# Two more landing buffers for gathered expert rows, in place of a spare pair of split activations

## The chip, the cores and the metric

The kernel runs on one core of one Trainium2 chip. A core has five engines that run side by side, each with its own instruction stream: TensorE (PE, matrix products), VectorE (DVE), ScalarE (ACT), GpSimd (POOL) and SyncE (SP). SP issues most transfers, POOL the indirect ones (gathers), ACT a few; 16 DMA engines carry them. The metric is device microseconds of one execution, as the median of several.

## The reference

One layer of a hybrid encoder on 1024 tokens of width 1024, in float32. A first half mixes tokens (a causal convolution and an RWKV-7 state recurrence side by side, one output projection, residual, layer norm). The second half is PEER: each token chooses 16 experts for each of 8 heads out of 16384, and every expert is one row of `peer_u` and one of `peer_v`. This change touches only that second half:

```
s1, s2 = q_first_half . peer_k1, q_second_half . peer_k2       # 128 scores each, for a token and head
cand   = top16(s1)[:, None] + top16(s2)[None, :]               # 256 sums
sc, ci = top_k(cand, 16);  expert = i1 * 128 + i2;  gate = softmax(sc)
z   = einsum('td,tkd->tk', h, peer_u[expert])                  # 128 experts a token
y2  = einsum('tk,tkd->td', gelu(z) * gate, peer_v[expert])
x   = layer_norm(ALPHA * x + gate2 * y2, ln2_g, ln2_b)
```

## The kernel before

The tokens lie in eight tiles of 128. Five of them (`DT`, tiles 0 to 4, 640 tokens) are done *densely*: every expert is computed for every token, and a gate matrix that was built earlier holds a zero where a token did not choose an expert. Three tiles (`GT`, 5 to 7) are done by *gathering*: for each of a token's 128 experts its row is fetched. Both run together in the last stage, from about 1350 us to the end; all that goes before is left as it was.

**The dense part** goes through 32 groups of four chunks of 128 experts. For a chunk, a tile of `peer_u` is loaded (`uraw`) and split into two fp32r halves, `uhi` by ACT (L1301) and `ulo` by POOL (L1303). PE forms 2 x 24 "up" products (L1387) into PSUM banks `mg`; ACT applies the gelu (L1389), VectorE multiplies with the gates (L1391), and the result is split into `ah` (ACT, L1392) and `al` (VectorE, L1393). These pairs are 640 wide and come from a ring of `ABUF` = 6. When a group's four chunks are through, 120 "down" products (L1403) with the split `peer_v` tiles (`vhi`, `vlo`, again L1301 and L1303) go into three PSUM banks `md` in turn, and VectorE adds each bank to an accumulator `yacc` (L1421). The last group (`finish`) adds its banks to the residual tiles `xres` instead (L1354), takes statistics (L1355), normalizes (ACT, L1360), and multiplies and adds the layer norm's rows (L1361, L1362).

**The gathered part** is a generator, `gather(t)`, of which a step is made after each chunk and down tile, so that 256 gathers a tile spread over the groups. One gather is an indirect DMA issued by POOL (L1258) that lands 128 rows of 4 KB, one for each token of the tile, in a buffer `grow`. The first 128 of a tile are rows of `peer_u`: VectorE multiplies with the tokens `gh` and sums into a column of `z` (L1266). The other 128 are rows of `peer_v`: VectorE adds the row times its weight to `gy` in PSUM (L1273). Gather `k` is written ahead of the use of gather `k - 4` (`AHEAD`), and the ring `grow` has `GBUF` = 6 buffers, which the tokens, the residual tile and rows for the layer norm also take in turn. After the last addition the tile is scaled (L1276), added to the residual (L1226), normalized, multiplied and added to (L1230 on VectorE, L1232 on POOL) and stored (L1233).

**The late choices.** For tiles 6 and 7 the choice of experts is made inside this stage, by VectorE, piece by piece after an accumulation (`choose_late`, lines 953 to 963, L823 to L827 and `choose`), in memory of a pool of its own, `lt`. A tile's choices are finished before its gathers begin; the last end when the gathers of the second tile are under way.

**What sets the order.** The program is written in the order of the loops, but the instructions of each engine are put in order by a scheduler that simulates the program with the framework's own costs and buffer counts. So a change of a buffer count moves instructions on all engines from the place on where it first counts. Each engine then works strictly in its order, and so does SP's queue of transfers.

Of the kernel before, what the change touches and what calls it, by code (L numbers as in the profile page):

```python
# [10 lines left out]
F32 = mybir.dt.float32  # L11
# [11 lines left out]
D = 1024  # L23
# [20 lines left out]
REGIONS = [(0, 2, 16), (2, 2, 8), (4, 4, 4), (8, 8, 1)]  # L44
NCAND = sum(m * w for _, m, w in REGIONS)
TB = 32
GBUF = 6
AHEAD = 4
NMM = 3
AHEADF = 11,  # L50
MERGE = 7,
# [25 lines left out]
CBUF = 4  # L77
GB = 2, 3
MB = 3
ABUF = 6  # L80
VBUF = 4

PH = 4
# [13 lines left out]
def layer_kernel(ctx, tc, x, cols, c_row, cond_w, w_in, w2a2, g2, w_out, ln_rows, wq, keys, peer_u, peer_ut, peer_v, peer_vt, out):  # L97
# [185 lines left out]
    def drain(gen):  # L283
        for _ in gen:
            pass
# [296 lines left out]
    turn = [0, 0, 0]  # L582
# [46 lines left out]
    side, rate, credit, fills = [], [0.0], [0.0], [0]  # L629
# [21 lines left out]
    kept, ys, late, normed, page2, st3, blocks = {}, {}, [], {}, [], [], [0]  # L651
# [169 lines left out]
    def best16(vs, ix, sm):  # L821

        V.max(vs[:, 0:8], sm)  # L823
        V.max_index(ix[:, 0:8], vs[:, 0:8], sm)
        V.match_replace(sm, vs[:, 0:8], sm, -3.0e38)
        V.max(vs[:, 8:16], sm)
        V.max_index(ix[:, 8:16], vs[:, 8:16], sm)  # L827
# [125 lines left out]
    def choose_late(tt, lt):  # L953

        for g in range(4):
            s = lt.tile([128, 512], F32, name="lscore")
            ld(s, score_d[tt][g])
            vi = lt.tile([128, 128], F32, name="lvi").rearrange("p (q h a r) -> p q h a r", q=2, h=2, a=2)
            val, idx = vi[:, 0], vi[:, 1].bitcast(U32)
            for m in range(4):  # L960
                best16(val[:, m // 2, m % 2], idx[:, m // 2, m % 2], s[:, 128 * m:128 * m + 128])
                yield
            yield from choose(tt, val, idx, 2 * g, 2, 2, lambda nm, d, w: lt.tile([128, w], d, name="l" + nm), V)
# [234 lines left out]
    df = ctx.enter_context(tc.tile_pool(name="df", bufs=1))  # L1198
    dy = ctx.enter_context(tc.tile_pool(name="dy", bufs=1))
    gp = ctx.enter_context(tc.tile_pool(name="gp", bufs=1, side="right"))  # L1200
    lt = ctx.enter_context(tc.tile_pool(name="lt", bufs=1, side="right"))
    psd = ctx.enter_context(tc.tile_pool(name="psd", bufs=PSD, space=PSUM))
    psy = ctx.enter_context(tc.tile_pool(name="psy", bufs=1, space=PSUM))

# [7 lines left out]
    def grow(dt=F32):  # L1212
        return gp.tile([128, D], dt, name="grow", bufs=GBUF)

    def bcast_row(src):
        r = grow()
        ld(r, src[None, :].to_broadcast([128, D]))
        return r

    def residual_norm(t, acc):  # L1220

        xt = grow()
        ld(xt, x1_d[t])
        for i in range(2):
            h_ = slice(512 * i, 512 * i + 512)
            V.scalar_tensor_tensor(xt[:, h_], xt[:, h_], ALPHA, acc(i), op0=OP.mult, op1=OP.add)  # L1226
        parts = [xt[:, 0:512], xt[:, 512:1024]]
        normalize(parts, parts)
        r = bcast_row(ln_rows[2])
        V.tensor_mul(xt, xt, r)  # L1230
        r = bcast_row(ln_rows[3])
        G.tensor_add(xt, xt, r)  # L1232
        ld(out[128 * t:128 * t + 128], xt)  # L1233

    late = {t: choose_late(t, lt) for t in score_d}

    def gather(t):
        if t in late:
            drain(late.pop(t))
        sel = []  # L1240
        for w in range(3):
            s = gp.tile([128, 128], F32, name=f"gsel{w}")
            ld(s, sel_d[t][w])
            sel.append(s)
        eid = gp.tile([128, 128], I32, name="eid", bufs=2)
        V.scalar_tensor_tensor(eid, sel[0], 128.0, sel[1], op0=OP.mult, op1=OP.add)

        hs = grow()
        ld(hs, h2_d[t])
        ht = psy.tile([128, D], F32, tag="ghy", name="gh")  # L1250
        A.activation(ht, hs, AF.Copy)
        z = de.tile([128, 128], F32, name="gz")
        yield
        pend = []
        for k in range(256 + AHEAD):
            if k < 256:
                r = grow()
                G.indirect_dma_start(out=r, out_offset=None, in_=peer_u if k < 128 else peer_v,  # L1258
                                     in_offset=bass.IndirectOffsetOnAxis(ap=eid[:, k % 128:k % 128 + 1], axis=0))
                pend.append(r)  # L1260
            i = k - AHEAD
            if i < 0:
                continue
            r = pend.pop(0)
            if i < 128:
                V.scalar_tensor_tensor(r, r, 1.0, ht, op0=OP.mult, op1=OP.mult, accum_out=z[:, i:i + 1])  # L1266
            elif i == 128:
                A.activation(z, z, AF.Gelu)
                V.tensor_mul(z, z, sel[2])
                y = psy.tile([128, D], F32, tag="ghy", name="gy")  # L1270
                V.tensor_scalar(y, r, z[:, 0:1], None, op0=OP.mult)
            else:
                V.scalar_tensor_tensor(y, r, z[:, i - 128:i - 127], y, op0=OP.mult, op1=OP.add)  # L1273
            yield
        r = bcast_row(mod_d[5].rearrange("a b -> (a b)"))
        V.tensor_mul(y, y, r)  # L1276
        residual_norm(t, lambda i: y[:, 512 * i:512 * i + 512])
        yield


    side[:] = [gather(t) for t in GT]
    n_side = len(side) * (256 + 2)
    done = [0]
# [83 lines left out]
    for g in range(32):  # L1367
# [6 lines left out]
        for e in range(4):  # L1374
# [5 lines left out]

            ah, al = (dl.tile([128, ND], F32R, name=n_, bufs=ABUF) for n_ in ("ah", "al"))
            for bs in NBLK:
                p = md(NW) if g == 0 and e < 3 and bs.start else mg(NW)
                i = 0
# [95 lines left out]
```

## Time and profile before

| | |
|---|---|
| three runs | 3143.58, 3144.41, 3155.35 us; median 3144.41 |
| profiled execution | 3149.86 us, its span 3148.1 us, mean granted clock 0.965 |
| busy, share of the span | PE 94%, weight loads 83%, DVE 76%, ACT 37%, POOL 58% |
| DMA | 945.77 MB, mean 300 GB/s; 768 gathers bring 402.70 MB of it |
| chain that ended last | PE 56%, DVE 21%, DMA 9%, issue 6%, POOL 4%, ACT 4% |

The page groups instructions by line: how often, busy time, mean ns of one, and the idle time of the engine before them with what ended it. Idle time of an engine that is not the bottleneck costs nothing, so the view to read is the one of a stretch of time with the waits of PE in it. Matmuls overlap: a product's own duration is longer than the time from one to the next.

### The profile page before, as it was taken

Reading aid. Unit: us, or ns where it says so; the run is one execution under the profiler, and the core shown is the slowest. Engines: PE = TensorE matmul, PEld = TensorE weight load, DVE = VectorE, ACT = ScalarE, POOL = GpSimd, SP = SyncE. Lnnn points to the kernel's source line nnn. Section 1 sums busy time; section 2 is a strip of 40 time slices with the busy share of each in tenths; the row PEclk is TensorE's granted clock in tenths of the full one; section 3 lists DMA queues with packets and bytes.
Section 4 is the critical chain, followed back from the end, with each engine's and each line's share of the span. In section 5 each row is a group of like instructions: output and inputs, shape, how many; then the busy total and the mean of one; then the engine's idle time right before and its main releaser. Section 6 shows DMA issues by size and latency. Waiting matters only on the chain.

```text
span 3148.1 us, 54845 instructions
## 1 busy us (share of the span) xinstructions
PE 2954.2 (94%) x20416; PEld 2609.6 (83%) x20416; DVE 2383.7 (76%) x5388; ACT 1179.6 (37%) x2220; POOL 1814.5 (58%) x1419
## 2 busy tenths in 40 slices
PE   6979999989799889999999999999999999999996
PEld 4748667878678788899889888899898998999985
DVE  6276764437876989379999998887787877778789
ACT  5562452434345667732323323323232232222323
POOL 2434112224352443487777766877787677787874
PEclk9989999968888999999999999999999999999998
DMA  8878857768665887899999998999999989999995
GB/s 317 308 204 302 265 171 216 261 230 307 201 241 209 322 322 285 315 350 338 325 335 327 323 324 306 343 341 334 342 341 340 343 308 343 327 343 337 337 335 199
DMA packets 431851, 945.77 MB, mean 300 GB/s; under 512 B 92464, under 2 KB 234208, under 8 KB 411104
## 3 DMA queue, kind: packets, MB, share of 16 engines
q1 hardware_dynamic: 318112, 497.62, 46.9%
q0 software_dynamic: 110592, 402.70, 34.6%
q10 hardware_dynamic: 2880, 41.94, 3.3%
q8 instruction: 160, 2.62, 0.3%
q14 instruction: 107, 0.88, 0.1%
HBM read 800.76 MB, written 141.39 MB: 299 GB/s over the span
## 4 chain that ended last, share of the span: by engine, by line
PE 56%; DVE 21%; DMA 9%; issue 6%; POOL 4%; ACT 4%; SPq 1%; POOLq 0%; DVEq 0%; ACTq 0%
PE md L1403 18%; PE mg L1387 18%; PE mm L217 8%; DVE grow L1266 2%; PE mm L867 2%; PE mm L525 2%; DMA vraw<-peer_vt 2%; DVE gy L1273 2%; POOL grow L1258 2%; DMA cw<-cond_w 1%; PE mgate L1105 1%; DVE yacc L1421 1%; DVE mask L1091 1%; DMA grow<-peer_v,eid 1%; POOL ulo L1303 1%
## 5 line engine op out<-in xcount | busy, mean ns | idle before, releaser
L1387 PE MATMUL mg<-h2h,uhi 128*128 128x320 f32 x2024 | 627.1, 310 | 7.4 <-DVE al L1393 7.4
L1387 PE MATMUL mg<-h2h,ulo 128*128 128x320 f32 x2024 | 626.0, 309 | 4.6 <-POOL ulo L1303 4.5
L1387 PE MATMUL mg<-h2l,uhi 128*128 128x320 f32 x2024 | 626.1, 309 | 0.0
L1273 DVE SCALAR_TENSOR_TENSOR gy<-grow,gz,gy 128x1024 f32<-128x1024 f32 x381 | 487.5, 1279 | 28.6 <-DMA grow<-peer_v,eid 23.7
L1266 DVE SCALAR_TENSOR_TENSOR grow<-grow,gh 128x1024 f32<-128x1024 f32 x384 | 461.1, 1211 | 49.1 <-DMA grow<-peer_u,eid 38.7
L1403 PE MATMUL md<-vlo,ah 128*128 128x512 f32 x1260 | 491.1, 391 | 0.0
L1403 PE MATMUL md<-vhi,al 128*128 128x512 f32 x1260 | 490.7, 390 | 0.0
L1403 PE MATMUL md<-vhi,ah 128*128 128x512 f32 x1260 | 485.9, 392 | 4.5 <-ACT ah L1392 3.4
L1258 POOL DMA_INDIRECT grow<-peer_v,eid x384 | 367.5, 957 | 165.1 <-DVE gy L1273 58.3
L1258 POOL DMA_INDIRECT grow<-peer_u,eid x384 | 362.5, 944 | 172.3 <-issue 59.4
L1387 PEld LDWEIGHTS mg<-h2h,uhi 128*128 128x128 f32 x2024 | 380.5, 188 | 16.4 <-DVE al L1393 11.1
L1387 PEld LDWEIGHTS mg<-h2h,ulo 128*128 128x128 f32 x2024 | 380.5, 188 | 9.0 <-POOL ulo L1303 6.2
L1387 PEld LDWEIGHTS mg<-h2l,uhi 128*128 128x128 f32 x2024 | 380.5, 188 | 5.1
L1303 POOL TENSOR_TENSOR vlo<-vraw,vhi 128x1024 fp32r<-128x1024 f32 x128 | 308.7, 2412 | 64.2 <-ACT vhi L1301 62.1
L1301 ACT ACTIVATE vhi<-vraw 128x1024 fp32r<-128x1024 f32 x128 | 135.3, 1057 | 536.4 <-DMA vraw<-peer_vt 497.7
L1303 POOL TENSOR_TENSOR ulo<-uraw,uhi 128x1024 fp32r<-128x1024 f32 x128 | 309.4, 2417 | 26.1 <-ACT uhi L1301 19.2
L1403 PEld LDWEIGHTS md<-vhi,ah 128*128 128x128 f32 x1260 | 235.8, 188 | 53.6 <-ACT ah L1392 5.4
L1403 PEld LDWEIGHTS md<-vlo,ah 128*128 128x128 f32 x1260 | 236.5, 188 | 49.1
L1421 DVE TENSOR_TENSOR yacc<-md,yacc 128x512 f32<-128x512 f32 x300 | 203.9, 684 | 96.3 <-PE md L1403 87.0
L1098 POOL TENSOR_TENSOR ob<-mask,selt 128x384 f32<-128x384 bf16 x160 | 140.2, 890 | 233.9 <-DVE mask L1091 96.5
L1403 PEld LDWEIGHTS md<-vhi,al 128*128 128x128 f32 x1260 | 236.5, 188 | 44.9
L205 POOL TENSOR_TENSOR wsplit<-wraw,wsplit 128x1024 fp32r<-128x1024 f32 x46 | 112.5, 2448 | 215.7 <-ACT wsplit L204 193.9
(415 smaller groups left out, 5747.6 us busy)
## 6 DMA issues: line engine op xcount, KB each, us to landing
uraw<-peer_ut SPq DMA_DIRECT2D x128, 512.0 KB
vraw<-peer_vt SPq DMA_DIRECT2D x128, 512.0 KB
wsplit<-split_wq SPq DMA_DIRECT2D x48, 1024.0 KB
G_d<-stage ACTq DMA_DIRECT2D x20, 2048.0 KB
gmat<-G_d SPq DMA_DIRECT2D x32, 1024.0 KB
cw<-cond_w SPq DMA_DIRECT2D x48, 512.0 KB
wsplit<-split_w_out SPq DMA_DIRECT2D x24, 1024.0 KB
split_w_in<-wsplit SPq DMA_DIRECT2D x22, 1024.0 KB
```

What stands on the lines that cost most here:

```text
L205: G.tensor_sub(lo, raw, hi.bitcast(F32))
L217: T.matmul(pt, l[:, k, :], r[k], start=i == 0, stop=i == 3 * KD - 1)
L525: T.matmul(pt[:, 128 * g:128 * g + 128], dg[:, 128 * j:128 * j + 128], ubuf[ct][:, g, LAGS - 1 - m:LAGS - 1 - m + 128], start=m == 0, stop ...
L1098: G.tensor_mul(ob[:, :3], mb[:, :3], gt[:, c:c + 3, None].to_broadcast([128, 3, 128]))
L1258: G.indirect_dma_start(out=r, out_offset=None, in_=peer_u if k < 128 else peer_v, in_offset=bass.IndirectOffsetOnAxis(ap=eid[:, k % 128:k ...
L1266: V.scalar_tensor_tensor(r, r, 1.0, ht, op0=OP.mult, op1=OP.mult, accum_out=z[:, i:i + 1])
L1273: V.scalar_tensor_tensor(y, r, z[:, i - 128:i - 127], y, op0=OP.mult, op1=OP.add)
L1301: A.activation(hi, raw, AF.Copy)
L1303: G.tensor_sub(lo, raw, hi.bitcast(F32))
L1387: T.matmul(p, l[:, k, :], r[k][:, bs], start=i == 0, stop=i == 3 * KD - 1)
L1403: T.matmul(p, l[:, ts], r[:, e % 2, :], start=e == 0 and q == 0, stop=e == 3 and q == 2)
L1421: ins = V.tensor_add(ya, p, ya)
```

## The change

`ABUF` goes from 6 to 5, which frees one `ah` and one `al`. `GBUF` goes from 6 to 7. `AHEAD` goes; the loop keeps `GBUF - 1` gathers written ahead, counted with the one that is used next, so five beyond it for four before. When the last late choice has been taken in the program (`late` is empty), its pool `lt` is closed and a pool `gq` with one buffer, `gland`, is opened in its place. From then on every eighth gather lands there, and six stand ahead.

```diff
-GBUF = 6
-AHEAD = 4
+GBUF = 7
...
-ABUF = 6
+ABUF = 5
...
-    lt = ctx.enter_context(tc.tile_pool(name="lt", bufs=1, side="right"))
+    ltx = ctx.enter_context(ExitStack())
+    lt = ltx.enter_context(tc.tile_pool(name="lt", bufs=1, side="right"))
...
+    more, turn = [], [0]
+
+    def landing():
+
+        if not late and not more:
+            ltx.close()
+            more.append(ctx.enter_context(tc.tile_pool(name="gq", bufs=1, side="right")))
+        turn[0] += 1
+        if more and turn[0] % (GBUF + 1) == 0:
+            return more[0].tile([128, D], F32, name="gland")
+        return grow()
...
-        pend = []
-        for k in range(256 + AHEAD):
-            if k < 256:
-                r = grow()
+        pend, k = [], 0
+        for i in range(256):
+            while k < 256 and len(pend) < GBUF - 1 + len(more):
+                r = landing()
                 G.indirect_dma_start(out=r, out_offset=None, in_=peer_u if k < 128 else peer_v,
                                      in_offset=bass.IndirectOffsetOnAxis(ap=eid[:, k % 128:k % 128 + 1], axis=0))
                 pend.append(r)
-            i = k - AHEAD
-            if i < 0:
-                continue
+                k += 1
             r = pend.pop(0)
```

No instruction is added or taken away; 53 of the 768 gathers land in `gland`, of which the first is gather 352. Up to the first down products of the first group every engine has the same order in both programs. From there it differs, in small moves all along. Line numbers of the changed program are lower by one up to the new function and higher by nine behind it (L1258 becomes L1269, L1303 becomes L1312).

The first place is POOL in a group of the third gathered tile (the 26th of the 32), from the `ulo` of its first chunk on. Before:

```order
L1303 TENSOR_TENSOR ulo<-uraw,uhi 128x1024
L1258 DMA grow<-peer_u,eid 128x1024 x6
L1303 TENSOR_TENSOR vlo<-vraw,vhi 128x1024
L1258 DMA grow<-peer_u,eid 128x1024 x6
L1303 TENSOR_TENSOR ulo<-uraw,uhi 128x1024
L1258 DMA grow<-peer_u,eid 128x1024 x3
L1303 TENSOR_TENSOR ulo<-uraw,uhi 128x1024
L1258 DMA grow<-peer_u,eid 128x1024 x3
L1303 TENSOR_TENSOR vlo<-vraw,vhi 128x1024
```

The same place in the changed program:

```order
L1312 TENSOR_TENSOR ulo<-uraw,uhi 128x1024
L1269 DMA grow<-peer_u,eid 128x1024 x3
L1269 DMA gland<-peer_u,eid 128x1024
L1269 DMA grow<-peer_u,eid 128x1024 x4
L1312 TENSOR_TENSOR vlo<-vraw,vhi 128x1024
L1269 DMA grow<-peer_u,eid 128x1024
L1312 TENSOR_TENSOR ulo<-uraw,uhi 128x1024
L1269 DMA grow<-peer_u,eid 128x1024 x2
L1269 DMA gland<-peer_u,eid 128x1024
L1269 DMA grow<-peer_u,eid 128x1024
L1312 TENSOR_TENSOR ulo<-uraw,uhi 128x1024
```

Eight gathers stand in one run for six, then one between `vlo` and the next `ulo` for six; after that they come by fours.

The second place is VectorE at the end, from the addition of one of PE's last banks to `xres` on. Before, the normalization of the last gathered tile (L231 to L245, L1230) stands behind the last of these additions:

```order
L1354 TENSOR_TENSOR xres<-md,xres 128x512
L1355 BN_STATS bnst<-xres 128x6 x3
L235 RECIPROCAL rstd<-rstd 128x1
L237 TENSOR_SCALAR bnmv<-bnmv 128x1
L235 RECIPROCAL rstd<-rstd 128x1
...
L1355 BN_STATS bnst<-xres 128x6
...
L1230 TENSOR_TENSOR grow<-grow 128x1024
L1361 TENSOR_TENSOR xres<-xres,gmat 128x512 x2
```

In the changed program it stands ahead of five of them; behind the last one comes a single statistic:

```order
L1363 TENSOR_TENSOR xres<-md,xres 128x512
L1364 BN_STATS bnst<-xres 128x6
L1230 TENSOR_TENSOR grow<-grow 128x1024
L1364 BN_STATS bnst<-xres 128x6
L1363 TENSOR_TENSOR xres<-md,xres 128x512 x2
...
L1363 TENSOR_TENSOR xres<-md,xres 128x512
L1367 SCALAR_TENSOR_TENSOR nbias<-bnmv,rstd 128x1
L234 RECIPROCAL rstd<-rstd 128x1
L236 TENSOR_SCALAR bnmv<-bnmv 128x1
L1370 TENSOR_TENSOR xres<-xres,gmat 128x512
L1364 BN_STATS bnst<-xres 128x6
```

The third place is SP's queue at the end. Before, the four last tiles of `peer_v` went out together:

```order
L1297 DMA uraw<-peer_ut 128x1024 x2
L1297 DMA vraw<-peer_vt 128x1024 x4
L1337 DMA xres<-x_d_107 128x1024
L1337 DMA xres<-x_d_109 128x1024
L1337 DMA xres<-x_d_105 128x1024
```

Now the fourth of them stands behind the gathered tile's scale row, its residual tile and a layer norm row, which wait for `grow` buffers:

```order
L1306 DMA uraw<-peer_ut 128x1024 x2
L1306 DMA vraw<-peer_vt 128x1024 x3
L1217 DMA grow<-mod_d 128x1024
L1223 DMA grow<-x_d_112 128x1024
L1217 DMA grow<-ln_rows 128x1024
L1346 DMA xres<-x_d_107 128x1024
L1306 DMA vraw<-peer_vt 128x1024
```

## The prediction

> **What bounds the kernel now.** I began with the stretches of the last stage, 1350 us to the end: busy time of each engine (its count of instructions in brackets), granted clock, DMA share, GB/s.
>
> ```profile
> core 0: us, PE busy (x) PEld busy (x) DVE busy (x) ACT busy (x) POOL busy (x), PEclk, DMA share, GB/s
> 1350.00:1700.00 350.00, 347.24 (x1936) 315.12 (x1936) 313.78 (x716) 104.93 (x174) 268.05 (x206) 1.00 0.94 334
> 1700.00:2100.00 400.00, 390.94 (x2178) 351.76 (x2177) 363.35 (x747) 117.99 (x195) 293.36 (x224) 1.00 0.93 325
> 2100.00:2500.00 400.00, 400.00 (x2233) 363.74 (x2232) 312.83 (x431) 104.34 (x171) 309.08 (x240) 1.00 0.95 342
> 2500.00:3050.00 550.00, 547.02 (x3075) 499.16 (x3074) 424.51 (x642) 150.73 (x247) 422.32 (x323) 1.00 0.93 335
> 3050.00:3121.00 71.00, 69.34 (x366) 60.92 (x364) 66.99 (x78) 15.73 (x26) 47.04 (x28) 1.00 0.71 254
> 3121.00:3148.00 27.00, 0.00 (x0) 0.00 (x0) 21.73 (x66) 9.81 (x18) 2.73 (x1) 0.58 0.31 117
> ```
>
> PE works 1754.55 of the 1771 us up to 3121; then follow 27 us without a matmul. VectorE is at 90% up to 2100 (313.78 of 350, 363.35 of 400), while the late choices run, and at 77 to 78% after. So the gathers, all of whose arithmetic is VectorE's, can cost time in two ways only: by making PE wait, or by leaving work for the 27 us. Next I read who waited, 1350 us to the end, PE and VectorE (us in total, times, longest), and the same for PE from 2100 to 3080 (last row).
>
> ```profile
> PE mg L1387 <- DVE al L1393: 7.4, 7, 1.7
> PE mg L1387 <- POOL ulo L1303: 4.5, 4, 2.1
> PE md L1403 <- ACT ah L1392: 3.4, 4, 1.3
> PE md L1403 <- DVE yacc L1421: 0.9, 2, 0.7
> ...
> DVE yacc L1421 <- PE md L1403: 87.0, 79, 4.0
> ...
> DVE grow L1266 <- DMA grow<-peer_u,eid: 38.7, 26, 6.2
> ...
> DVE gy L1273 <- DMA grow<-peer_v,eid: 23.7, 21, 4.3
> ...
> PE mg L1387 <- POOL ulo L1303: 3.0, 3, 2.1
> ```
>
> VectorE waits 38.7 + 23.7 = 62.4 us for gathered rows, but PE's waits add up to 7.4 + 4.5 + 3.4 + 0.9 = 16.2 us. That is the ceiling of what better gathering can give before 3121: 62 us of waiting on an engine with room costs PE at most 16. Between 2100 and 3080, with the late choices gone, PE waits 3.0 us and only for `ulo`; so nearly all waits for `al`, `ah` and `yacc` lie where VectorE is full of other work, too.
>
> **The change part by part.** *Lead of a gather.* Before, four gathers stand issued beyond the one being used; now five, and six once the late choices are done. In 2100 to 3050 POOL issued 239 + 186 = 425 gathers in 950 us, 2.24 us apiece:
>
> ```profile
> L1258 POOL DMA_INDIRECT grow<-peer_v,eid x239 | 225.0, 942 | 89.6 <-DVE gy L1273 38.3 <-issue 37.9 <-DVE al L1393 2.2
> L1258 POOL DMA_INDIRECT grow<-peer_u,eid x186 | 175.1, 942 | 68.1 <-issue 33.3 <-DVE grow L1266 23.8 <-DVE mg L1391 3.6
> ```
>
> The lead is thus some 4 x 2.24 = 9.0 us before, 11.2 and 13.4 after. Landings on the chain of waits (start, duration), the third row a weight load for below:
>
> ```profile
> 1634.40 9.69 DMA grow<-peer_v,eid
> 1686.14 6.26 DMA grow<-peer_v,eid
> ...
> 2659.59 14.28 DMA vraw<-peer_vt
> ```
>
> A landing of 6.26 fits the old lead and one of 9.69 doesn't; both fit the new ones. I expect the 62.4 us of VectorE's waits to fall to 20 to 35. (The Trainium skill, "DMA: Bandwidth & Descriptors", section "Anatomy of one DMA", gives 2.0 us plus bytes over 436 GB/s; for 512 KB that would be 3.2 us, an estimate by that page, and no lead would ever be short. The rows of 6.26 and 9.69 on DMA engines that are 93 to 95% busy speak against it; it comes back as a rival.)
>
> What PE gets of this: of the waits for `al`, `ah` and `yacc` (11.7 us) I take 2 us. Lower bound 0, if the late choices alone cause them, upper 11.7. I choose near the lower end because they sit where VectorE is at 90%, and because the gathers it no longer waits for are only pulled into the same full stretch.
>
> *POOL's order.* The longest wait of PE looks like this (PE, VectorE and POOL in order of time; in brackets the idle time before and what ended it):
>
> ```profile
> 2687.24 0.41 PE L1387 MATMUL mg<-h2h,ulo 128*128 128x320 f32 x1 [2.08 <-POOL ulo L1303]
> ...
> 2682.82 1.22 DVE L1266 SCALAR_TENSOR_TENSOR grow<-grow,gh 128x1024 f32<-128x1024 f32 x1 [3.14 <-DMA grow<-peer_u,eid]
> ...
> 2675.08 2.40 POOL L1303 TENSOR_TENSOR vlo<-vraw,vhi 128x1024 fp32r<-128x1024 f32 x1 [7.53 <-ACT vhi L1301]
> 2677.64 0.95 POOL L1258 DMA_INDIRECT grow<-peer_u,eid  x1 [0.15 <-issue]
> 2678.89 0.94 POOL L1258 DMA_INDIRECT grow<-peer_u,eid  x1 [0.30 <-DVE grow L1266]
> ```
>
> A weight tile landed late (14.28 us), POOL stood 7.53 us before `vlo`, then issued six gathers before the `ulo` that PE wanted; meanwhile VectorE starved 3.14 us. In the new order of such a group eight gathers go out before that `vlo` and one, not six, stands between it and `ulo`: five issues of 0.94 + 0.30 = 1.24 us, 6.2 us, are gone from `ulo`'s way, three times the 2.08 us. Of the 4.5 us for `ulo` I take 3, that is the three waits up to 3080. Bounds: 4.5 gained; on the other side the second rival.
>
> *VectorE's order* shifts by one to four steps: gathers' additions now stand ahead of the `yacc` additions that free PSUM. At 1279 ns each, four are 5.1 us of delay:
>
> ```profile
> L1273 DVE SCALAR_TENSOR_TENSOR gy<-grow,gz,gy 128x1024 f32<-128x1024 f32 x381 | 487.5, 1279 | 28.6 <-DMA grow<-peer_v,eid 23.7
> ...
> 2429.68 13.66 PE md L1403 x60
> ```
>
> Twelve such products fill one bank: 13.66/5 = 2.73 us, and three banks are in turn, 8.2 us; VectorE moreover waits 87.0 us in those places for PE. I cost this at 0. Were that cover gone, the added wait would be at most 5.1 us for a group.
>
> *The pairs of activations, 6 to 5.* A group of four chunks holds four pairs until its last product with `peer_v`. A fifth takes the next group's first chunk; the second chunk's pair is written after 48 further up-products, which in PE's order stand behind all 120 down-products of the old group. So nobody waits: 0. Without that order, the wait would be for the rest of a down stage, at most two halves of 13.66 us.
>
> *Opening the eighth buffer* makes one gather wait for the last reader of the late choices' memory; that gather goes out after the choices have ended in VectorE's order and five others are ahead of it (11.2 us). 0, at most 1.
>
> *The end.* VectorE's groups in 3121 to 3148 (count | busy us, mean ns | idle before), then from the timeline PE's last product, VectorE's last piece and POOL's last:
>
> ```profile
> L1361 DVE TENSOR_TENSOR xres<-xres,gmat 128x512 f32<-128x512 f32 x10 | 8.8, 898 | 0.8 <-ACT xres L1360 0.8
> L1362 DVE TENSOR_TENSOR xres<-xres,gmat 128x512 f32<-128x512 f32 x10 | 6.6, 680 | 0.0
> L1355 DVE BATCH_NORM_STATS2 bnst<-xres 128x6 f32<-128x512 f32 x4 | 2.5, 679 | 0.0
> L1230 DVE TENSOR_TENSOR grow<-grow 128x1024 f32<-128x1024 f32 x1 | 1.2, 1226 | 1.2 <-ACT grow L247 1.2
> ...
> 3120.59 0.39 PE L1403 MATMUL md<-vlo,ah 128*128 128x512 f32 x1
> ...
> 3143.47 1.28 DVE L1362 TENSOR_TENSOR xres<-xres,gmat 128x512 f32<-128x512 f32 x2
> ...
> 3128.56 2.73 POOL L1232 TENSOR_TENSOR grow<-grow 128x1024 f32<-128x1024 f32 x1 [21.66 <-DVE grow L1230]
> ```
>
> In the new order the last gathered tile is normalized ahead of PE's last outputs. Behind the last of them stand the same 20 products and sums of `xres`, but one statistic for four (1.9 us less), no L1230 (1.2 and its wait of 1.2), and POOL's sum L1232 comes early, beside which L1361 took 898 ns for L1362's 680 (2.2 less). That is 6.5 us off the 27. It can come off only if VectorE has room for it before 3121: 71 - 66.99 = 4.0 us of idle time, and some three gathers that have moved ahead of this stretch (3 x 1.28 = 3.8), 7.8 in all. Against it: the last tile of `peer_v` is now issued on SP behind three row loads that wait for landing buffers, and its VectorE multiply stands in line with the tail; a landing like the 14.28 us above holds VectorE perhaps 4 us. I take 4 gained; bounds 7.8 gained, 4 lost.
>
> Sum: 2 + 3 + 4 = 9 us, against the profiled execution's own 3149.86 us (span 3148.1, 1.8 around it): 3140.9. That execution stands 5.4 us above the median of the runs shown, so for the median I take 3144.4 - 9 = 3135.
>
> **The rivals.**
> *All of it:* the 16.2 us vanish and the end gives 7.8: 3144.4 - 24 = 3120. For it: every kind of wait has a VectorE or POOL that was itself late. Against: the late choices' stretch stays full.
> *Nothing:* PE's waits stay (late choices), and the end is VectorE's total work, which no buffer shortens: 66.99 of 71 us busy. 3144.
> *Bursts hold the weights up (the other side):* a down stage now begins with seven or eight gathers in one run on POOL, before six. Each is 512 KB, at 335 GB/s 1.6 us of DMA, and 1.24 us of POOL; two more delay the weight tile and `vlo` by 2.5 to 3.2 us.
>
> ```profile
> L1303 POOL TENSOR_TENSOR ulo<-uraw,uhi 128x1024 fp32r<-128x1024 f32 x128 | 309.4, 2417 | 26.1 <-ACT uhi L1301 19.2 <-issue 4.8
> ```
>
> `ulo` is late for PE today 4 times in 128, so most groups absorb that. If eleven of the 31 groups pay one wait of the 2.08 us seen: +23 - 6 = +17, 3161. It decides from three groups on, where 3 x 2.08 eats the 4 + 2 us gained elsewhere. Against it: `ulo` is now nearer to the burst, as above.
> *The gathers were never short of lead:* a landing always fits four steps, so the new buffers do nothing, and only the end's order gives its 4 to 5 us: 3140. The 62.4 us of waits speak against it. By the page's 3.2 us (the Trainium skill, "DMA: Bandwidth & Descriptors", as above) it would come out so.
>
> **How the numbers follow.** Forecast 0.45 (3135, own range 3127 to 3142), all of it 0.20, nothing 0.20, lead never short 0.05, bursts 0.10. The range 3119 to 3152 leaves out the ends of the first and the last rival. This measurement tells about 0.5% from no change, 15.7 us: faster means below 3128.7, slower above 3160.1. Faster: most of "all of it" (0.19) and the forecast's low end (0.08), 0.27; slower: 0.06, a good half of "bursts"; within: 0.67.
>
> **What would show it.** Right: VectorE's waits for gathered rows under 35 us; PE's waits near 11, those for `ulo` under 2; less than 24 us between PE's last product and the end; busy PE time unchanged. Wrong: waits for `al` as before with gather waits gone (then the late choices were the cause); `ulo` waits above 8 us behind runs of eight gathers; or VectorE stopped in the end for `vraw`.

## The result and the profile after

The changed kernel takes 3130.88 us (median of 6 runs, 3125.62 to 3132.74); the kernel before 3147.41 us (6 runs, the three shown above among them, 3139.68 to 3155.35). The medians differ by 16.5 us, 0.52%; the ratio that the record estimates from all these runs is 0.9928 [0.9905, 0.9951], so the change is faster, by little. The time lies in the forecast's own range and 4 us under the predicted 3135. It stands above the 3128.7 that I drew for "faster" from the earlier median; against the kernel before as it ran here, 16.5 us is just past the 15.7 behind that bound. "Faster" had 0.27 and "within" 0.67. The profiled execution took 3130.84 us, its span is 3129.1.

The stretches of the last stage of the changed kernel; columns as in the same view of before:

```profile
core 0: us, PE busy (x) PEld busy (x) DVE busy (x) ACT busy (x) POOL busy (x), PEclk, DMA share, GB/s
1350.00:1700.00 350.00, 345.26 (x1922) 313.58 (x1921) 318.62 (x709) 104.47 (x173) 267.95 (x206) 1.00 0.94 335
1700.00:2100.00 400.00, 397.64 (x2219) 360.68 (x2219) 376.55 (x764) 121.77 (x198) 300.78 (x230) 1.00 0.95 336
2100.00:2500.00 400.00, 400.00 (x2240) 364.33 (x2239) 315.20 (x428) 103.60 (x170) 305.02 (x235) 1.00 0.95 341
2500.00:3050.00 550.00, 550.00 (x3089) 501.68 (x3088) 432.81 (x648) 148.94 (x244) 430.17 (x329) 1.00 0.94 338
```

From 2100 to 3050 PE is now busy without a break (950 of 950 us; before 947.02). While the late choices run, VectorE does more than before in the same time (376.55 of 400 for 363.35), because it waits less. What is left of PE's and VectorE's waits, 1340 us to the end (us in total, times, longest):

```profile
PE mg L1396 <- DVE al L1402: 6.1, 5, 2.3
PE mg L1412 <- DVE xres L1363: 1.4, 1, 1.4
PE md L1412 <- ACT vhi L1310: 1.0, 1, 1.0
PE mg L1396 <- issue: 0.5, 1, 0.5
PE md L1412 <- DVE yacc L1430: 0.4, 1, 0.4
...
DVE grow L1275 <- DMA grow<-peer_u,eid: 15.7, 9, 5.9
...
DVE gy L1282 <- DMA grow<-peer_v,eid: 3.2, 3, 2.1
```

VectorE waits 18.9 us for gathered rows where it waited 62.4. PE's waits fell from 16.4 to 9.6 us, small ones that the view leaves out included; `ulo` and `ah` are gone from the list, `al` mostly stays, and the last two tiles bring two waits that were not there, for `vhi` and `xres`.

The end, from the timeline: PE's last product, POOL's last sum of the gathered tile, VectorE's last piece.

```profile
3108.47 0.39 PE L1412 MATMUL md<-vlo,ah 128*128 128x512 f32 x1
...
3103.80 2.40 POOL L1232 TENSOR_TENSOR grow<-grow 128x1024 f32<-128x1024 f32 x1 [7.45 <-DVE grow L1230]
...
3124.46 1.28 DVE L1371 TENSOR_TENSOR xres<-xres,gmat 128x512 f32<-128x512 f32 x2
```

PE ends at 3108.9, 20.2 us before the span does (27.1 before), and the gathered tile's last sum stands ahead of that, not behind. The groups of VectorE in these 20.2 us:

```profile
L1370 DVE TENSOR_TENSOR xres<-xres,gmat 128x512 f32<-128x512 f32 x10 | 6.8, 688 | 0.3 <-ACT xres L1369 0.3
L1371 DVE TENSOR_TENSOR xres<-xres,gmat 128x512 f32<-128x512 f32 x10 | 6.6, 682 | 0.0
L1364 DVE BATCH_NORM_STATS2 bnst<-xres 128x6 f32<-128x512 f32 x2 | 1.4, 684 | 0.0
L1363 DVE TENSOR_TENSOR xres<-md,xres 128x512 f32<-128x512 f32 x2 | 1.4, 682 | 0.0
```

L1230 is gone from it, the multiplications by `gmat` take 688 ns for 898, and two statistics are left for four. VectorE is busy 16.49 us in this stretch, 21.73 in that of before; the ten products and ten sums of `xres` stand in both.

**Three pieces.** I cut every profiled execution at two points: the first product with `peer_v` (row "md<-vhi,ah") and the end of PE's last product. Ahead of the first point PE's order is the same in every kernel here. For the two profiled executions: 1333.5 + 1787.4 + 27.1 us before, 1331.3 + 1777.5 + 20.2 after. So of 19.0 us less, 9.9 are the stage, 6.9 the end, and 2.2 lie where nothing was changed.

### The profile page after: what moved, and what is told of

Its sections match the earlier page's. It is cut to its first block, busy times and chain, and to the rows that moved or that the text cites. A ratio compares the mean times of both kernels' runs of the same rounds, so it can differ in the third digit from the quotient of the medians.

```text
span 3129.1 us, 54818 instructions
## 1 busy us (share of the span) xinstructions
PE 2959.5 (95%) x20416; PEld 2618.7 (84%) x20416; DVE 2392.4 (76%) x5388; ACT 1182.9 (38%) x2220; POOL 1816.8 (58%) x1419
## 4 chain that ended last, share of the span: by engine, by line
PE 66%; DVE 19%; DMA 7%; issue 3%; ACT 3%; POOL 1%; SPq 1%; DVEq 0%; ACTq 0%; POOLq 0%
PE mg L1396 24%; PE md L1412 23%; PE mm L216 8%; PE mm L524 2%; DMA cw<-cond_w 2%; PE mm L866 2%; DVE mask L1090 1%; DVE gy L1282 1%; PE mgate L1104 1%; DVE grow L1275 1%; PE bank L703 1%; DVE cw L299 1%; DVE yacc L1430 1%; PE bank L729 1%; PE bank L671 1%
## 5 line engine op out<-in xcount | busy, mean ns | idle before, releaser
L1282 DVE SCALAR_TENSOR_TENSOR gy<-grow,gz,gy 128x1024 f32<-128x1024 f32 x349 | 446.6, 1280 | 4.3 <-DMA grow<-peer_v,eid 3.2
L1275 DVE SCALAR_TENSOR_TENSOR grow<-grow,gh 128x1024 f32<-128x1024 f32 x363 | 435.9, 1211 | 17.1 <-DMA grow<-peer_u,eid 15.7
L1269 POOL DMA_INDIRECT grow<-peer_u,eid x363 | 343.7, 947 | 171.1 <-issue 60.5
L1269 POOL DMA_INDIRECT grow<-peer_v,eid x352 | 334.9, 951 | 164.6 <-DVE gy L1282 67.5
L1312 POOL TENSOR_TENSOR vlo<-vraw,vhi 128x1024 fp32r<-128x1024 f32 x128 | 308.9, 2413 | 37.0 <-ACT vhi L1310 34.8
L1312 POOL TENSOR_TENSOR ulo<-uraw,uhi 128x1024 fp32r<-128x1024 f32 x128 | 309.8, 2420 | 20.6 <-ACT uhi L1310 18.1
L1398 ACT ACTIVATE mg<-mg 128x320 f32<-128x320 f32 x253 | 106.9, 423 | 348.9 <-PE mg L1396 330.9
```

The costliest lines, as they stand in the source:

```text
L1312: G.tensor_sub(lo, raw, hi.bitcast(F32))
L1398: A.activation(p, p, AF.Gelu)
```

## The experiments

All runs, each compared with the kernel before on the same chip; then, of its profiled execution, the start of the first product with `peer_v`, the time from there to the end of PE's last product, from there to the end, and PE's waits in the stage.

| run | time, ratio [95%] | first product | stage | end | PE waits |
|---|---|---|---|---|---|
| before | | 1333.5 | 1787.4 | 27.1 | 16.4 |
| the change | 3130.88, 0.9928 [0.9905, 0.9951] | 1331.3 | 1777.5 | 20.2 | 9.6 |
| again | 3129.95, 0.9944 [0.9920, 0.9969] | 1332.0 | 1779.3 | 20.2 | 9.7 |
| third time | 3131.28, 0.9948 [0.9928, 0.9967] | 1329.5 | 1778.7 | 20.2 | 10.5 |
| five pairs alone | 3146.75, 0.9991 [0.9975, 1.0007] | 1326.2 | 1785.8 | 27.1 | 12.1 |
| seven throughout | 3131.11, 0.9948 [0.9928, 0.9967] | 1328.2 | 1779.0 | 21.3 | 11.5 |
| seven, again | 3137.09, 0.9962 [0.9943, 0.9980] | 1333.5 | 1779.3 | 21.2 | 11.1 |
| six, one more late | 3148.44, 0.9998 [0.9980, 1.0016] | 1338.0 | 1781.0 | 24.6 | 13.4 |
| six, one more early | 3145.26, 0.9986 [0.9968, 1.0004] | 1320.7 | 1784.2 | 27.1 | 14.4 |
| nine | 3141.67, 0.9969 [0.9956, 0.9983] | 1328.0 | 1784.6 | 20.1 | 14.5 |
| last normalization held back | 3125.97, 0.9919 [0.9892, 0.9946] | 1336.1 | 1780.4 | 22.7 | 10.8 |
| no late choices, six | 3114.56, 0.9885 [0.9856, 0.9913] | 1341.6 | 1767.1 | 17.4 | 3.3 |
| the same, again | 3119.25, 0.9910 [0.9886, 0.9933] | 1324.9 | 1768.3 | 17.4 | 3.4 |
| no late choices, eight | 3118.13, 0.9897 [0.9870, 0.9925] | 1336.8 | 1764.6 | 19.6 | 0.9 |

The third column is the noise of the times: it moves by 21 us, with PE's instructions ahead of it in the same order. The end repeats to 0.1 us wherever the order is repeated (27.1 twice, 20.2 three times, 21.3 and 21.2, 17.4 twice), the stage to 2 in these pairs. So I read stage and end from the profiles, and from the times only whether they go along.

**Where in the stage.** Every profile here records 9884 products of PE from that first point on, so stage and end can also be cut by their count: at product 4400, some 30 us behind the last late choice, and at product 9452, just ahead of the last group (us):

| order | to product 4400 | from there to 9452 | from there to the end |
|---|---|---|---|
| before; five pairs | 799.4, 800.1 | 903.2, 898.9 | 112.0, 114.0 |
| six, one more late | 796.4 | 897.4 | 111.7 |
| the change, three times | 793.5, 795.2, 794.6 | 897.5 each | 106.8 each |
| last normalization held back | 798.0 | 897.5 | 107.7 |
| seven throughout, twice | 792.0, 792.2 | 897.5, 897.6 | 110.8, 110.7 |
| six, one more early | 797.6 | 901.7 | 112.0 |
| nine | 794.9 | 899.4 | 110.4 |
| no late choices, six | 782.9, 785.4 | 900.5, 899.1 | 101.2, 101.2 |
| no late choices, eight | 782.6 | 898.6 | 102.9 |

Up to some 780 us the run with one more late has the order of before, and the runs with seven and with the normalization held back have that of the change. So this first piece has three executions of the old order, mean 798.6, and six of the new, mean 794.3. That is 4.4 us, and the least certain of the three, since executions of one order differ by up to 6.0. Behind it the change takes 897.5 us each time, without a wait of PE, and the old order 1.4 and 5.7 us more. The last piece is 5 to 7 us shorter.

### Five pairs of activations, and nothing else

In the kernel before:

```diff
-ABUF = 6
+ABUF = 5
```

> The kernel before with only the ring of split activations cut from 6 to 5 pairs. Theory (the fifth pair is never waited for, since the second chunk's pair is written behind all down products): the time of before, within 3 us, and PE's waits for ah and al as before (10.8 us). Rival (the spare pair was in use): 5 us or more slower, with PE or ScalarE waiting where a pair comes free.

Measured: 0.9991 [0.9975, 1.0007], and the built order of instructions is that of the kernel before, row by row. The sixth pair was never needed; it cost nothing to give away. That makes this run a second execution of the old order, and it corrects a reading. PE's and VectorE's waits in it:

```profile
PE mg L1387 <- DVE al L1393: 7.4, 9, 1.7
PE md L1403 <- ACT ah L1392: 1.7, 1, 1.7
PE mg L1387 <- POOL ulo L1303: 1.3, 3, 0.7
...
DVE gy L1273 <- DMA grow<-peer_v,eid: 46.9, 43, 4.0
...
DVE grow L1266 <- DMA grow<-peer_u,eid: 29.9, 30, 4.0
```

VectorE waits for gathered rows even more (76.8 us), but `ulo` costs PE 1.3 us, not 4.5, and the wait of 2.08 us at 2687, from which I had argued POOL's part, is not there.

### Seven buffers throughout, without the eighth

The change, with the old loop and its written lead, `lt` opened as before and no `landing()`:

```diff
+AHEAD = 5
...
-            while k < 256 and len(pend) < GBUF - 1 + len(more):
-                r = landing()
+        for k in range(256 + AHEAD):
+            if k < 256:
+                r = grow()
```

> Seven landing buffers and five pairs, without the eighth buffer. Theory (a longer lead of the gathers, and the end's order, make the gain): the end gives its 5 to 7 us, the last stage another 5 to 7 us: 11 to 14 us faster than before, VectorE's waits for gathered rows 25 to 40 us (62 before, 19 with the whole change). Rival (the eighth buffer is what counts, since PE's only waits past the late choices are for POOL's ulo): only the end's 5 to 7 us.

Measured: stage and end together 1800.3 us, before 1814.5, the change 1797.8. The seventh buffer makes most of it. VectorE waits 15.5 + 2.9 us for gathered rows, as with the eighth (25.4 in the second execution). To size the eighth, the same kernel ran again beside the changed one:

> Seven landing buffers throughout, five pairs, no eighth, a second time, beside the changed kernel on the same chip. Theory, the seventh buffer makes nearly all of the gain: 1800 us from the first product with peer_v to the end as in its first look (the changed kernel: 1798 and 1800), and a time within 3 us of the changed kernel's in the same call. Rival, the eighth buffer carries a third of it or more (it cuts into the waits after the late choices): 5 us or more slower than the changed kernel.

> The changed kernel once more, as the partner of the run with seven buffers. Theory: 20.2 us from PE's last product to the end as in both looks so far, 1777 to 1780 us from the first product with peer_v to PE's last, no wait of PE for ulo; 0.993 to 0.995 of the kernel before. Rival, that those looks were lucky: the end 22 us or more, or waits for ulo as before.

Measured: 1800.5 us against 1798.9 in the profiles (on the means of all executions 1800.4 for seven and 1798.7 for the change). These sums make the eighth too small. Up to product 4400 both kernels have nearly the same order (the first difference is 783 us in), so that the 2 us by which seven is ahead there look like chance; from there to the last group both take 897.5 us; the last piece takes 110.8 and 110.7 us with seven and 106.8 with the change. So the eighth is worth some 4 us, all of it in the last group and the end. The times differ by 5.8 us (3137.09 and 3131.28), where 3 or less stood as the theory and 5 or more as its rival; the two ratios' intervals overlap ([0.9943, 0.9980] and [0.9928, 0.9967]), and on the first chip seven buffers took 3131.11, so the times do not settle it. The changed kernel repeated its stage, its end, and had no wait for `ulo` a third time.

### One more buffer late only, early only

Late only, in the changed kernel: six landing buffers until the late choices are done, then seven.

```diff
-GBUF = 7
+GBUF = 6
...
-ABUF = 5
+ABUF = 6
```

Early only is the kernel before with five pairs and `landing()`, the extra buffer in a pool of its own ahead of `lt`, used as long as choices are pending:

```diff
+        more[:] = [gq] if late else []
+        turn[0] += 1
+        if more and turn[0] % (GBUF + 1) == 0:
+            return more[0].tile([128, D], F32, name="gland")
+        return grow()
```

> Six landing buffers and six pairs as before, with the one more buffer in the memory of the late choices: seven from gather 352 on. Theory (lead): up to 2100 us as before, from there on no wait of PE for ulo (3 us) and the end shorter by 4 to 6 us: 7 to 9 us faster than before. Rival (the gain is made in the stretch of the late choices): within 4 us of before.

> The mirror of the run with the eighth alone: six buffers and one more only while the late choices are still to come, then six. Theory (the last stage's gain is made while the late choices fill VectorE): PE's waits between the groups 8 and 13 fall from 9.1 and 5.1 us (two looks at the order before) to about 2.5 as with seven throughout, and the stretch up to the last product is 1778 to 1782 us; its end stands in the order of before, so from the last product to the end it takes 27 us: 6 to 8 us faster than before. Rival (the later groups count): 0 to 3 us.

Measured, late only: stage 1781.0, end 24.6, together 9 us under before, but a time of 0.9998 [0.9980, 1.0016], which allows 6 us at most. About 3 of the 9 us lie ahead of product 4400, where the order is nearly all the old one, and look like chance. Behind it the run takes 897.4 us, as the change does, and its last piece, 111.7, is near that of before. The time shows none of this. Early only: the end is that of before, 27.1, as expected; the stage, 1784.2, is 2 us over the expected 1778 to 1782, and the time is unchanged. Two waits of 2.3 us stand in it where the changed kernel has none, the first still among the late choices, the second after them, when the ring is back at six:

```profile
2001.60 0.41 PE L1395 MATMUL mg<-h2h,uhi 128*128 128x320 f32 x1 [2.31 <-DVE al L1401]
...
2559.89 0.42 PE L1395 MATMUL mg<-h2h,uhi 128*128 128x320 f32 x1 [2.32 <-DVE al L1401]
```

So neither half alone is worth what seven buffers from first to last are. With seven or more behind the late choices PE has no wait at all in the chunks from there to 3050 us, in seven of seven profiled executions (seven throughout twice, the change three times, the normalization held back, one more late).

### Nine

In the changed kernel, with room made by a further pair; nine buffers after the late choices:

```diff
-GBUF = 7
+GBUF = 8
...
-ABUF = 5
+ABUF = 4
```

> The change carried one step on: four pairs of activations, eight landing buffers, nine once the late choices are done. Theory: VectorE's waits for gathered rows fall from 19 to under 10 us, but PE's waits are down to 9 us already and mostly the late choices' own, so 0 to 4 us faster than the changed kernel (3127 to 3131). Rival (bursts): runs of nine gathers hold weight tiles up and PE waits for ulo again, 5 us or more slower than the changed kernel. Rival (pairs): with four pairs the next group's first chunk waits for the old group's last down products, some us in each of 31 groups.

Measured: VectorE waits 8.4 us for rows, half of the changed kernel's; 0.9969 [0.9956, 0.9983], less than the change gains. Stage and end take 6.0 us more than the change's mean. PE's waits, and one of ScalarE that the changed kernel does not have:

```profile
PE mg L1396 <- DVE al L1402: 6.1, 6, 2.2
PE md L1412 <- DVE xres L1363: 3.2, 1, 3.2
PE md L1412 <- ACT ah L1401: 2.8, 1, 2.8
PE mg L1412 <- DVE xres L1363: 1.3, 1, 1.3
...
ACT ah L1401 <- PE md L1412: 158.0, 20, 18.1
```

Of the 6.0 us, 3.7 are lost between product 9452 and PE's last: there PE waits 3.2 + 1.3 = 4.5 us for additions to `xres`, where the change waits 1.4, and 1.0 for `vhi`. ScalarE now waits 158.0 us for pairs that down products still read, as the rival had it, but PE's one wait for `ah` goes back to VectorE instead. More lead buys nothing more, although VectorE's waits fall by another half; whether the loss comes from four pairs or from the new order was not separated.

### Without the late choices

If VectorE's waits cost PE only where VectorE is full, they must cost nothing with the choices gone. The kernels of this section leave out the choices for tiles 6 and 7, whose gathers read those of tile 5; that is 600 instructions of VectorE fewer, and another order on every engine. In the kernel before:

```diff
-    late = {t: choose_late(t, lt) for t in score_d}
+    late = {}
...
-            ld(s, sel_d[t][w])
+            ld(s, sel_d[GT[0]][w])
```

> The kernel before without the late choices: tiles 6 and 7 gather with the choices of tile 5, and VectorE's work for choosing is left out (some 450 small instructions, so its own time is no version of the kernel). Theory (with room on VectorE, six buffers are enough for PE): PE's waits for al, ah and yacc fall from 11.7 to under 3 us although VectorE still waits for gathered rows by 30 us or more. Rival (the short lead itself hurts PE): the waits stay at 8 us or more.

Measured: VectorE still waits 42.1 + 17.8 = 59.9 us for rows, PE 3.3 us in all, 2.0 of them for `al` and `ah`. The sharper test is the change on top of this, beside a second execution of the base:

> The kernel before without the late choices, a second time, as the base of the next run on the same chip (gathered tiles 6 and 7 read the choices of tile 5, so the part of the computation that chooses for them is left out). Both theories expect what its first look showed, but for the stretch ahead of the first product with peer_v, which varied by 20 us over the looks so far: about 1767 us from that product to PE's last, and 17.4 us from there to the end; PE's waits for al, ah and yacc near 2 us while VectorE waits about 60 us for gathered rows. Time 3108 to 3122.

> The changed kernel without the late choices (the same part left out; both new landing buffers are there from the start of the gathers). Theory, waits for gathered rows cost PE only where the late choices fill VectorE: PE's waits were 2 to 3 us without the choices and six buffers, so eight buffers may take away some 40 of VectorE's 60 us of waits and give PE no more than 2 to 3; the end is VectorE's backlog, and in this order ten products and sums of xres stand behind the last bank's addition for twelve with six buffers, 1.4 us less: the stretch from the first product with peer_v to the end shorter by 2 to 5 us than with six, ratio to it 0.998 to 1. Rival, more buffers shorten the stage by themselves: 8 to 10 us less in the stage as with the late choices there, and 7 less at the end, 15 to 17 in all, ratio about 0.995.

VectorE's groups of the additions with six buffers, and then with eight, 1340 to 3090 us:

```profile
L1273 DVE SCALAR_TENSOR_TENSOR gy<-grow,gz,gy 128x1024 f32<-128x1024 f32 x381 | 488.5, 1282 | 43.6 <-DMA grow<-peer_v,eid 37.7 <-issue 3.6 <-DVE gy L1273 0.3
L1266 DVE SCALAR_TENSOR_TENSOR grow<-grow,gh 128x1024 f32<-128x1024 f32 x383 | 459.8, 1213 | 64.0 <-DMA grow<-peer_u,eid 59.2 <-issue 4.1
```

```profile
L1282 DVE SCALAR_TENSOR_TENSOR gy<-grow,gz,gy 128x1024 f32<-128x1024 f32 x333 | 426.4, 1280 | 1.5 <-DMA grow<-peer_v,eid 0.2
L1275 DVE SCALAR_TENSOR_TENSOR grow<-grow,gh 128x1024 f32<-128x1024 f32 x336 | 403.3, 1212 | 22.2 <-issue 15.3 <-DMA grow<-peer_u,eid 5.7 <-DVE yacc L1430 0.4
```

Measured: 96.9 us of waits for rows become 7.1 (5.9 in these rows, 1.2 for a row in `gland`; besides, 15.3 for which the profile names nothing, 7.7 before). That is more than the change saves with the choices there, and stage and end go from 1785.7 to 1784.1 us (1784.5 in the first execution with six): 1 us. The times say the same, 3119.25 and 3118.13. The rival had 15 to 17 us. The two executions with six agree: VectorE waited 59.9 and 96.9 us, PE 3.3 and 3.4, and the stage took 1767.1 and 1768.3. So where VectorE is 76 to 79% busy, as it is here from 1350 to 3050 us, its waits for rows hardly reach PE. The stage did give the 2 to 3 us that PE still waited.

This does not show that all of the change's 15 us needs the late choices. Only the 4.4 us up to product 4400 lie where the choices fill VectorE. The old order's 5.7 and 1.4 us behind it lie where VectorE is 77 to 78% busy; PE's waits there are 3.0 us for `ulo` in the one execution, with half clock behind the longest, and 1.1 us in the other, 0.6 of it for `ulo`. The end gains 6.9 us there and loses 2.1 here, by the place of VectorE's last work in each order. Nor does the sum of VectorE's waits tell what PE pays: in the old order 62.4 and 76.8 us went with a stage of 1787.4 and 1785.8. And each size of the ring also gives each engine another order; no run here changes the lead and keeps the order, so the two were not separated.

The end did not come out as expected, 19.6 us for 16: PE ends earlier, VectorE does not, and its last addition of a bank stands 6 us behind PE's last product:

```profile
3101.04 0.39 PE L1412 MATMUL md<-vlo,ah 128*128 128x512 f32 x1
...
3107.61 0.69 DVE L1363 TENSOR_TENSOR xres<-md,xres 128x512 f32<-128x512 f32 x1
```

### The end: does the last normalization's place set it?

The change again, and the change with the normalization of the last gathered tile, its L1230 and L1232 held behind the last addition to `xres`:

```diff
+        if t == GT[-1]:
+            yield
+        with tc.issue_after(last_add[0].ins) if t == GT[-1] else nullcontext():
...
-                V.tensor_add(xt[:, hs], p, xt[:, hs])
+                last_add[:] = [V.tensor_add(xt[:, hs], p, xt[:, hs])]
```

> The changed kernel unaltered, for a second profile beside runs of before on the same chip. The looks so far differ by up to 12 us in the part ahead of the last stage, whose order no edit touched (first down product at 1326 to 1338 us), so stretches are compared and not spans. Theory: from the first down product to the last product 1777 to 1780 us (before 1787 and 1786), from there to the end 20 us (before 27 and 27), time 14 to 20 us under before. Rival (the gain was a lucky draw of both medians): under 8 us.

> The changed kernel with one edit in the last group: the last gathered tile's normalization may only be issued once PE's last output has been added, as it stood in the order before. Theory (the end's gain is this order): the time from PE's last product to the end goes from 20 back to 25 to 28 us, all else as changed: 5 to 7 us slower than the changed kernel. Rival (the end is shorter because the gathers end earlier): 20 to 22 us, as fast as the changed kernel.

Measured: 20.2 us again; 22.7 with the normalization behind. The theory said 25 to 28, the rival 20 to 22. The edit does not bring back the old order, though. The normalization now stands almost last on VectorE, and POOL's sum behind it; the old order had L1230 ahead of all ten products by `gmat` of this stretch, and POOL's sum beside the first two:

```profile
3131.30 1.22 DVE L1233 TENSOR_TENSOR grow<-grow 128x1024 f32<-128x1024 f32 x1
...
3132.59 2.72 POOL L1235 TENSOR_TENSOR grow<-grow 128x1024 f32<-128x1024 f32 x1 [26.93 <-DVE grow L1233]
```

So the products by `gmat` take 686 ns here, as in the change. The edit also shortens PE's last group (84.9 us from product 9452 for 86.6), so that last group and end together are only 0.9 us longer than the change's. The time (3125.97, ratio 0.9919) shows no loss. What the end's gain is made of is better read from the rows of both ends: products by `gmat` 8.8 and 6.8 us, statistics 2.5 and 1.4, L1230 with its wait 2.4 and none. That is 5.5 of the 6.9 us; the rest, in smaller rows and waits, was not separated.

## Why the prediction was right, and where its sum was not

The direction and the two places were right, and in the main the mechanism: rows that VectorE no longer waits for, fewer waits of PE, less work behind its last product. One term of the stage came out by luck, and the sum was too small. It said 9 us: 5 for the stage and 4 for the end. The old order's two executions average 1786.6 us of stage and 27.1 of end, the changed order's three 1778.5 and 20.2: 8.1 + 6.9 = 15.0 us. The times say 16.5, 18.6 and 17.2.

- **The lead.** VectorE's waits for rows were to fall from 62.4 us to 20 to 35. They fell to 18.9, 20.2 and 20.9. But "four, five, six ahead" came from the code. The built order of the changed kernel does not move by a row if the written lead is held at five, nor does that of the kernel before with a written lead of five for four: the order is the same, so the scheduler does not go by the written lead. What counts is the ring, six, seven or eight.
- **`al`, `ah`, `yacc`, taken as 2 of 11.7 us.** Measured 11.7 and 9.7 before, 6.5, 7.1 and 8.0 after: 3.5 us on the means (the run with the normalization held back, of the same order up to there, has 9.6, and with it the gain is 2.9). Right in kind (`al` mostly stays, and so do the late choices), a little small.
- **`ulo`, taken as 3 of 4.5 us.** 4.5 and 1.3 before, none in three executions after: 2.9 us on the means. The size came out by luck, the reasoning did not: I built it on one wait of 2.08 us that the same order does not have in its second execution. A landing that is late once is not a property of the order.
- **Waits that came.** 1.0 us for `vhi` and 1.4 for `xres`, near the end, in all three executions; neither was in the sum. The last tile of `peer_v` behind the three row loads on SP, of which I had warned, is neither: VectorE has no wait for `vraw`. What held `vhi` up is shown in the last section.
- **What the sum lacked in the stage.** PE's waits fell by 4.3 us on the means, the stage by 8.1. A wait can also cost more than its own length, which I left off every one: after some of them PE's products run at half pace. Here is a wait of the changed kernel and the stretches behind it (PE busy, granted clock, DMA share, GB/s):

```profile
1666.63 0.42 PE L1396 MATMUL mg<-h2h,uhi 128*128 128x320 f32 x1 [2.35 <-DVE al L1402]
...
1667.35 0.47 PE L1396 MATMUL mg<-h2h,uhi 128*128 128x320 f32 x1
1667.61 0.47 PE L1396 MATMUL mg<-h2l,uhi 128*128 128x320 f32 x1
1667.88 0.47 PE L1396 MATMUL mg<-h2h,ulo 128*128 128x320 f32 x1
```

```profile
core 0: us, PE busy (x), PEclk, DMA share, GB/s
1664.00:1667.00 3.00, 0.65 (x4) 0.99 0.81 286
1667.00:1670.00 3.00, 3.00 (x13) 0.50 0.82 290
1670.00:1673.00 3.00, 3.00 (x18) 0.94 0.93 303
```

The clock is at 0.50 for 3.4 us, products stand 0.265 us apart for 0.147, and some 1.6 us are lost, two thirds of the wait once more. Adding up, over the stage, what the distance between products exceeds its usual 0.147 and 0.228 us by where no wait is shown and the excess is over 30%, gives 4.5 and 7.2 us for the old order and 2.9, 4.6 and 3.3 for the new: 2.2 us less on the means. About half of that is half clock, and that half looks like chance: the old order has one and three such stretches, the new one has one, two and one, the run with one more late none and the one with the normalization held back two. Some 1.6 us of the 8.1 I cannot assign.
- **The end, taken as 4 us, bounds 7.8 gained and 4 lost.** 6.9 gained. The step that was mis-sized is the discount. I had counted 6.5 us of work that goes from behind PE's last product, and took 4 because VectorE might lack the room ahead of it or be stopped by the late `peer_v` tile; neither happened. The count fits the rows: statistics 1.1 us for the 1.9 counted, L1230 and its wait 2.4 for 2.4, products beside POOL's sum 2.0 for 2.2, 5.5 in all. The run with the normalization held back (2.5 us of the end lost) neither bears that out nor refutes it, since it does not restore the old order.
- **Costs at nothing.** Five pairs for six: right, shown alone. The additions ahead of `yacc`: right, 0.9 and 0.6 us of PE's waits in the old order, 0.4, none and 1.1 in the new. Opening the eighth: no wait of its own was seen.
- **Rivals.** "Bursts hold the weights up" is out: no wait of PE for `ulo` behind seven or eight gathers in a run, three executions. "Never short of lead", which the Trainium skill's "DMA: Bandwidth & Descriptors", section "Anatomy of one DMA", would give, is out as well: VectorE's waits fell by two thirds. "Nothing" held that PE's waits for `al` would stay with the late choices; most did, but not enough for its 3144. "All of it" was too far in the stage, and near in the end. The measured time lies between it and the forecast.

## What to carry to other kernels

An engine's sum of waits does not price them: 97 us of VectorE's waits were worth 1 us where it had slack all along. Read its share of busy time beside its waits, by stretch, and then the bound engine's own waits. Size a ring of landing buffers by trying one more and one more again: here seven gave most of the gain, the eighth some 4 us, and a ninth, bought with a pair of activations, lost 6. Before arguing from one long wait, see whether a second execution of the same order has it. Cut stretches at counts of the bound engine's instructions, so that noise ahead of a change is not taken for its effect.

## What the hardware showed that I had not expected

**Half clock after a short wait.** In the profiled executions with the late choices, from none to three waits of PE in the stage (of five to nine of 0.9 us or more) are followed by the half-clock stretch above. A wait of 2.35 us brings it in the first execution of the changed kernel; in the third the wait at the same place is 2.49 us and does not. In the run with five pairs 1.03 and 0.69 us in quick succession are enough:

```profile
3067.52 0.42 PE L1387 MATMUL mg<-h2h,uhi 128*128 128x320 f32 x1 [1.03 <-DVE al L1393]
3067.77 0.31 PE L1387 MATMUL mg<-h2l,uhi 128*128 128x320 f32 x1
3068.77 0.42 PE L1387 MATMUL mg<-h2h,ulo 128*128 128x320 f32 x1 [0.69 <-POOL ulo L1303]
```

The Trainium skill, "TensorE: Matmul & The Clock Gate", section 'Part 1: The HAM clock gate (the "warmup" mystery)', describes a free-running window of 3.4 us and a half-rate clock after an idle one. The half rate, its length and that it comes to the same wait once and not another time agree. That an idle window is needed does not: here waits of 1.0 + 0.7 us and of 2.35 us sufficed, and the measurement decides.

**VectorE beside POOL.** The wait for `vhi` goes back to VectorE's multiplication of a weight tile, two inputs in SBUF, that took 5.68 us where the same line took 1.22 five microseconds earlier. POOL's `ulo` and `vlo` run beside it from 3069.11 to 3073.90:

```profile
3064.58 1.22 DVE L1308 TENSOR_TENSOR vraw<-vraw,gmat 128x1024 f32<-128x1024 f32 x1
3069.30 5.68 DVE L1308 TENSOR_TENSOR vraw<-vraw,gmat 128x1024 f32<-128x1024 f32 x1
...
3069.11 2.43 POOL L1312 TENSOR_TENSOR ulo<-uraw,uhi 128x1024 fp32r<-128x1024 f32 x1
3071.48 2.42 POOL L1312 TENSOR_TENSOR vlo<-vraw,vhi 128x1024 fp32r<-128x1024 f32 x1
...
3075.02 1.06 ACT L1310 ACTIVATE vhi<-vraw 128x1024 fp32r<-128x1024 f32 x1 [3.32 <-DVE vraw L1308]
```

The Trainium skill, "SBUF — State Buffer", section "Who interferes with whom", says that a VectorE instruction with two inputs in SBUF contends with a POOL instruction that reads SBUF; these rows agree, and give the price: VectorE ended 1.08 us after the second POOL instruction, so it stood for nearly the whole of both. The two later executions of the change have the same 5.69 and 5.68 us. The multiplications of gathered rows have one input in SBUF only (`gh` is in PSUM) and take 1.21 us with or without POOL beside them.

**The same order, 21 us apart.** The first product with `peer_v` came at 1320.65 us in one profiled execution (one more buffer early) and at 1341.61 in another (no late choices, six), with PE's instructions ahead of it the same:

```profile
1320.65 0.39 PE L1411 MATMUL md<-vhi,ah 128*128 128x512 f32 x1
```

```profile
1341.61 0.39 PE L1403 MATMUL md<-vhi,ah 128*128 128x512 f32 x1
```

That is more than the whole effect of the change. What makes it was not looked into. Whoever compares two profiled executions of this kernel has to cut them at that point first.
